# Up stage of a trunk layer: token blocks transposed before their sums, and three output sums of the early pairs on VectorE

## The chip, the cores and the metric

One NeuronCore of one Trainium2 chip runs the whole layer in a single launch. The metric is the device time of one execution, in microseconds (us). The time before the change is the median of three runs, 1518.04 us (1517.04 to 1518.28).

The engines are named as in the profile: PE is TensorE (PEld its weight load), DVE is VectorE, ACT is ScalarE, POOL is GpSimd, SP is SyncE, which here only issues DMAs.

## The reference, cut to what matters

One layer of a hybrid encoder: 16 meta tokens and 1024 tokens of width 1024. An input projection feeds neighbourhood attention and a gated recurrence; the two are merged, projected by `w_o`, and added to the residual stream. An MLP follows. The change lies between the two last steps:

```python
mix = jax.nn.sigmoid(gate_na) * y_na + jax.nn.sigmoid(gate_hg) * y_hg
h = h + mix @ w_o[l]
m = rms_norm(h, norm_mlp[l])
h = h + jnp.square(jax.nn.relu(m @ w_up[l])) @ w_down[l]
...
h = rms_norm(h, norm_final)
return h[:, N_META:]
```

`w_up` is 1024 x 4096 and `w_down` is 4096 x 1024; everything is float32. Only the 1024 token rows pass through these last steps.

## The kernel before, in words

**Precision.** Every large product is made from operands split into a rounded part `hi` (a cast on ACT) and a remainder `lo` (a subtraction on DVE), with three matmuls per block: hi·hi, hi·lo and lo·hi. In `chain` these are the lines L918, L919 and L920, twelve matmuls of 128x128 by 128x512 for one product.

**The `w_o` stage.** The token rows are eight blocks of 128 rows, `hres[0]` to `hres[7]`. `wo_rows(i, hc)` makes one half of a block's product with `w_o` (24 matmuls on L122 to L124) and adds it into `hres[i]` on DVE (L1216). `row_scale(i)` sends the sum to DRAM from the ACT queue (L1237, tile `hsp`), squares it on ACT (L1238) and makes the root on POOL (L92, L93). `scale_row(i)` multiplies the block in place on DVE (L1243); it has to wait until the DMA has read the old values.

**Winograd form.** The product with `w_up` is made in Strassen-Winograd form: the normalised rows, transposed, form a 2x2 grid of blocks `b11`, `b21` (rows 0 to 511, the two halves of the columns) and `b12`, `b22` (rows 512 to 1023). Beside these the scheme needs four sums, `t1` to `t4`. `row_sums(j)` makes those of block j and block j+4 from rows: two subtractions on DVE (L1249, L1250) and two on POOL (L1251, L1252). `to_variant` then transposes one 128x512 piece on PE (four transposes, L1259, into a PSUM bank `pt`), casts it from PSUM on ACT (L1261) and takes the remainder on DVE, again from PSUM (L1262). There are seven variants (`b11`, `b21`, `b22`, `t1` to `t4`) of four pieces each: 28 pieces and 112 transposes. The first eight pieces (`b11`, `b21`) are turned inside the `w_o` stage, the other twenty between the first products of the up stage. `b22` and `t2` go to a new tile `nT1`, which takes the place of the `w_o` operand `mT[1]`.

**The up stage.** `w_up` is taken in 16 pairs of 128-column blocks; a pair takes seven products, of one chain each. For pairs 0 to 2 ("early") the first two products are made ahead (`product_1` of the three, then `product_2` of the three), and the transposes above are laid between their matmuls. A pair's weights are its own sums on DVE (`pair_sums`, L908 to L911), then split by ACT (L1308) and DVE (L1309). The results go through relu and square on ACT (L1313, L1314), and `pair_out` with `finish_u2` makes four sums of them (`block_out`, L1401) for the next stage, on POOL except in the last pair, each followed by a DMA from SP (L1402). `load_pair` (L1335, SP) loads the weights of the pair after next.

**What sets the order.** In the `w_o` stage the framework's scheduler places the instructions. The up stage is under `manual_schedule`: there each engine runs in the order in which the code is written. All engines run in order and meet at semaphores.

Of the kernel before, what the change touches and what calls it, by code (L numbers as in the profile page):

```python
# [9 lines left out]
F32 = mybir.dt.float32  # L10
# [3 lines left out]
ALU = mybir.AluOpType  # L14
# [4 lines left out]
P = 128  # L19
# [3 lines left out]
TH = 512  # L23
# [25 lines left out]
def layer(ctx: ExitStack, tc: tile.TileContext, x, meta, w_in, w_na, w_hg, w_o, w_up, w_dn,  # L49
          g_mix, g_mlp, g_fin, gain, bias, lbl, lmask, wmask, out):  # L50
    nc = tc.nc
    pe, act, dve, pool, sp = nc.tensor, nc.scalar, nc.vector, nc.gpsimd, nc.sync
# [20 lines left out]
    def bank(tag, name):  # L73
        return banks[tag].tile([P, 4, P], F32, tag=tag, name=name)
# [4 lines left out]
    ident = cp.tile([P, P], F32, name="ident")  # L79
# [7 lines left out]
    def mm_tile(n=512, name="mm"):  # L87
        mm_cycle.append(mm_cycle.pop(0))
        return bank(mm_cycle[-1], name).rearrange("p a b -> p (a b)")[:, :n]
# [40 lines left out]
    def u_tiles(h, name):  # L130
        return [up.tile([P, KC, UW[h]], F32R, tag=f"u{h}{i}", name=f"{name}{h}{i}") for i in range(2)]
# [615 lines left out]
    with (tc.tile_pool(name="npr", bufs=1, side="right", reuse_waits="tile") as npr,  # L747
# [18 lines left out]
        for p in range(NPAIR):  # L766
            NB = npl.tile([P, 2, 1024], F32, tag="NB", name="NB")
            for i in range(2):
# [3 lines left out]
                for o, j0, m in ((0, 0, 3), (432, 1, 2), (720, 0, 2)):  # L772
                    a = NB[:, i, o:o + m * SW].rearrange("p (j c) -> p j c", c=SW)[:, :, :P]
                    pool.tensor_tensor(a, a, bs[:, j0 * P:(j0 + m) * P].rearrange("p (j c) -> p j c", c=P),
                                       op=ALU.subtract)
# [41 lines left out]
            for b in (0, 4, 8):  # L817
                pt = bank("t", "vpt")
                m = min(4, 9 - b)
                for j in range(m):  # L820
                    pe.transpose(pt[:, j], vT[:, b + j], ident)
                src = pt[:, :m].rearrange("p j (i d) -> p j i d", i=2)
# [331 lines left out]
    for br, wsrc in enumerate((w_hg, w_na)):  # L1154
        for jj in range(0, KC, 2):
            hi, lo = ahead_w.pop() if ahead_w else branch_weights(wsrc, jj)
            if br == 0 and jj == 2:
                list(branch_operand(1))
            for j in (jj, jj + 1):
# [4 lines left out]
                for h in range(2):  # L1164
                    pm = mm_tile()
                    t = slice(h * TH, (h + 1) * TH)
                    for k in range(4):
                        c = slice(k * 2 * P + (j - jj) * P, k * 2 * P + (j - jj + 1) * P)
# [33 lines left out]
    hres = [None] * 8  # L1202
# [39 lines left out]
    def scale_row(i, rs):  # L1242
        dve.scalar_tensor_tensor(hres[i], hres[i], rs, g2, op0=ALU.mult, op1=ALU.mult)  # L1243

    def row_sums(j):

        b11, b21, b12, b22 = (hres[i][:, q:q + TH] for i in (j, j + 4) for q in (0, TH))
        t2 = rowp.tile([P, TH], F32, tag="t2", name="t2", bufs=3)
        dve.tensor_tensor(b11, b12, b11, op=ALU.subtract)  # L1249
        dve.tensor_tensor(t2, b22, b11, op=ALU.subtract)  # L1250
        pool.tensor_tensor(b12, b22, b12, op=ALU.subtract)  # L1251
        pool.tensor_tensor(b21, b21, t2, op=ALU.subtract)  # L1252
        return {"t1": b11, "b22": b22, "t3": b12, "t2": t2, "t4": b21}

    def to_variant(tag, src, var, j):

        pt = bank(tag, "pt") if tag else mm_tile().rearrange("p (a b) -> p a b", a=4)
        for k in range(4):
            pe.transpose(pt[:, k], src[:, k * P:(k + 1) * P], ident)  # L1259
        hi = var[0][:, :, j * P:(j + 1) * P]  # L1260
        act.copy(hi, pt)  # L1261
        dve.tensor_tensor(var[1][:, :, j * P:(j + 1) * P], pt, hi.bitcast(F32), op=ALU.subtract)  # L1262

    for i in range(4):
        for hc in range(2):
            wo_rows(i, hc)
        scale_row(i, row_scale(i))
    nT0 = u_tiles(0, "nT")
    nV = {"b11": [t[:, :4, :TH] for t in nT0], "b21": [t[:, 4:, :TH] for t in nT0]}
    nB = []  # L1270
    for i in range(4, 8):
        for hc in range(2):
            wo_rows(i, hc)
        if i < 6:
            for j in (2 * i - 8, 2 * i - 7):
                to_variant("a", hres[j][:, :TH], nV["b11"], j)
                to_variant("a", hres[j][:, TH:], nV["b21"], j)
        if i < 7:
            scale_row(i, row_scale(i))
            if i > 4:  # L1280
                nB += [row_sums(j) for j in range(len(nB), i - 3)]
    wos.close()
    wps.close()


    ups = ExitStack()
    upw = ups.enter_context(tc.tile_pool(name="upw", bufs=1, reuse_waits="tile"))
    nT1 = u_tiles(1, "nT")
    nV["b22"], nV["t2"] = [t[:, :4, :TH] for t in nT1], [t[:, 4:, :TH] for t in nT1]
    nvp = ups.enter_context(tc.tile_pool(name="nvp", bufs=1, reuse_waits="tile"))  # L1290
    for v in ("t1", "t3", "t4"):
        nV[v] = [nvp.tile([P, 4, TH], F32R, name=f"n{v}{q}") for q in range(2)]
# [58 lines left out]
    def pair_sums(q):  # L1351
        raw = q.raw
        A = q.A = {"a11": raw[:, :4, :P], "a12": raw[:, 4:, :P], "a21": raw[:, :4, P:], "a22": raw[:, 4:, P:]}
        for v in ("s1", "s3"):
            t = a_tile(upw, "sx", bufs=2, n=D).rearrange("p (k c) -> p k c", c=P)
            A[v], A["s" + str(int(v[1]) + 1)] = t[:, :4], t[:, 4:]
        winograd(dve, *(A[v] for v in ("a11", "a12", "a21", "a22", "s1", "s2", "s3", "s4")))
# [12 lines left out]
    def product_1(q, w=None, between=lambda k: None, tag="pa"):  # L1370
        q.p1, q.u11 = a_tile(upa, "p1", bufs=EARLY), a_tile(upa, "u11", bufs=EARLY)
        q.pa = up_bank(tag)
        chain(q.pa, w or q.W["a11"], nV["b11"], True, between)
        act.copy(q.p1, q.pa)

    def product_2(q, w=None, between=lambda k: None):
        chain(q.pa, w or q.W["a12"], nV["b21"], False, between)
        relu2(q.u11, q.pa)
        (act if q.early or q.last else sp).dma_start(usp[0][q.m][:, 0], q.u11)
# [18 lines left out]

    def block_out(q, v, a, b, op, dst):
        q.S[v] = a_tile(upb, "us", bufs=4)  # L1400
        (dve if q.last else pool).tensor_tensor(q.S[v], a, b, op=op)  # L1401
        (pool if q.last else sp).dma_start(dst, q.S[v])  # L1402

    def product_7(q, then):
# [7 lines left out]
    def pair_out(q):  # L1412

        block_out(q, 2, q.u11, q.u1, ALU.subtract, usp[2][q.m][:, 1])
        block_out(q, 0, q.u1, q.u3, ALU.add, usp[1][q.m][:, 1])
        block_out(q, 1, q.S[0], q.u11, ALU.subtract, usp[1][q.m][:, 0])
# [16 lines left out]
    def last_first_weights(k):  # L1433
        if k == 2:
            first_w[2].append(weights(first_raw[2][:, 4:], upf))
# [6 lines left out]
    with tc.manual_schedule(engines={e.engine for e in (pe, act, dve, pool, sp)}):  # L1442

        rs7 = row_scale(7)
        count = [0]

        def transposes(n):
            for n in range(count[0], count[0] + n):
                v = ("t1", "b22", "t3", "t2", "t4")[n % 5]
                to_variant("a", nB[n // 5][v], nV[v], n // 5)  # L1450
                count[0] += 1

        product_1(pairs[0], first_w[0][0], lambda k: transposes(k > 0))
        first_weights(2, 0)
        transposes(2)
        scale_row(7, rs7)
        product_1(pairs[1], first_w[1][0], lambda k: transposes(1))
        transposes(1)
        nB.append(row_sums(3))
        product_1(pairs[2], first_w[2][0], lambda k: transposes(1), "mm")  # L1460
        transposes(2)
        product_2(pairs[0], first_w[0][1], lambda k: (transposes(1), last_first_weights(k)))
        rows_.close()
        hress.close()

        rawp = ups.enter_context(tc.tile_pool(name="rawp", bufs=1, side="right", reuse_waits="tile"))
        upr = ups.enter_context(tc.tile_pool(name="upr", bufs=1, side="right", reuse_waits="tile"))
        load_pair(0)
        load_pair(1)
        pair_sums(pairs[0])  # L1470
        product_2(pairs[1], first_w[1][1])
        next_weights(-1, "s4", "s2")
        product_2(pairs[2], first_w[2][1])
        early_w.close()
        psum_pools(pc=2, pb=2, pa=2)
        upb = ups.enter_context(tc.tile_pool(name="upb", bufs=1, reuse_waits="tile"))
        w_pools.insert(0, upr)
        next_weights(-1, "s1", "s3", "a22")
        for m, q in enumerate(pairs):
            if m + 2 < NP + 2:  # L1480
                load_pair(m + 2)
            (product_3 if q.early else product_1)(q)
            if m == 0:
                product_6(q)
            if m + 1 < NP:
                pair_sums(pairs[m + 1])
            if m:
                product_4(pairs[m - 1])
            if q.early:
                if m:  # L1490
                    product_6(q)
                next_weights(m, "a11", "s4")
                if m:
                    finish_u2(pairs[m - 1])
                next_weights(m, "a12", "s2", "s1")
            else:
                finish_u2(pairs[m - 1])
                product_3(q)
                next_weights(m, "a11", "s4")
                product_2(q)  # L1500
                next_weights(m, "a12", "s2")
                product_6(q)
                next_weights(m, "s1")
            product_5(q, lambda: next_weights(m, "s3"))
            product_7(q, lambda: next_weights(m, "a22"))
            if not q.last:
                pair_out(q)
        product_4(pairs[-1])
        finish_u2(pairs[-1])
        next_step()  # L1510
# [328 lines left out]
```

## Time and profile before

| | |
|---|---|
| median of three runs | 1518.04 us |
| the profiled execution, its own time | 1516.13 us |
| its span, first to last instruction | 1514.3 us |
| PE busy | 1499.2 us, 99% |
| DVE busy | 1033.6 us, 68% |
| ACT busy | 656.8 us, 43% |
| POOL busy | 381.7 us, 25% |
| mean granted clock of PE | 0.999 |
| `w_o` rows, first to last add (L1216) | 806.3 to 884.9 us of the span |
| early products and transposes | 884.0 to 909.7 us |
| early pairs, up to pair 3 | 909.7 to about 966 us |

A row of the timeline reads: start in us from the span's start, length in us, engine, line, operation, output and inputs by the program's names, shapes, and the count of merged instructions; in square brackets stands how long the engine had been idle, and what ended that. A row of the chain of waits has start, length and the line that time is put down to. A group's row has, behind the bar, busy us and mean ns of one, then the idle time before them. Matmuls overlap: one starts every 0.23 us though each shows 0.39 us, so distances between starts are what counts on PE.

### The profile page before, as it was taken

Reading aid. Unit: us, or ns where it says so; the run is one execution under the profiler, and the core shown is the slowest. Engines: PE = TensorE matmul, PEld = TensorE weight load, DVE = VectorE, ACT = ScalarE, POOL = GpSimd, SP = SyncE. Lnnn points to the kernel's source line nnn. Section 1 sums busy time; section 2 is a strip of 40 time slices with the busy share of each in tenths; the row PEclk is TensorE's granted clock in tenths of the full one; section 3 lists DMA queues with packets and bytes.
Section 4 is the critical chain, followed back from the end, with each engine's and each line's share of the span. In section 5 each row is a group of like instructions: output and inputs, shape, how many; then the busy total and the mean of one; then the engine's idle time right before and its main releaser. Section 6 shows DMA issues by size and latency. Waiting matters only on the chain.

```text
span 1514.3 us, 23574 instructions
## 1 busy us (share of the span) xinstructions
PE 1499.2 (99%) x9248; PEld 1255.7 (83%) x9248; DVE 1033.6 (68%) x1612; ACT 656.8 (43%) x1170; POOL 381.7 (25%) x358
## 2 busy tenths in 40 slices
PE   9999999999999999999999999999999999999998
PEld 8888888888888888888888887888888888888886
DVE  7876666656786796665584468877777445877876
ACT  7131313136575576344132145555555534334444
POOL 3313131324414400110000214444444200231142
PEclk9999999999999999999999999999999999999999
DMA  4211011113213237444655124544444576563224
GB/s 170 59 29 57 29 53 33 44 36 125 90 60 95 98 96 252 145 152 172 213 167 208 42 91 151 183 153 153 151 146 162 201 248 234 188 233 111 98 84 153
DMA packets 142590, 195.60 MB, mean 129 GB/s; under 512 B 8192, under 2 KB 90368, under 8 KB 142480
## 3 DMA queue, kind: packets, MB, share of 16 engines
q1 hardware_dynamic: 133072, 172.34, 34.4%
q10 hardware_dynamic: 7232, 14.44, 2.5%
q0 software_dynamic: 2176, 7.34, 1.3%
q8 instruction: 72, 1.18, 0.3%
q14 instruction: 38, 0.31, 0.1%
HBM read 139.56 MB, written 54.53 MB: 128 GB/s over the span
## 4 chain that ended last, share of the span: by engine, by line
PE 88%; DVE 6%; issue 2%; ACT 2%; DMA 1%; POOL 0%; POOLq 0%; ACTq 0%; DVEq 0%
PE mm L122 11%; PE mm L123 11%; PE mm L124 11%; PE mm L1514 4%; PE pa L1514 4%; PE pb L918 4%; PE pc L1514 4%; PE pb L919 4%; PE pb L1514 4%; PE pb L920 4%; PE pc L920 3%; PE pc L919 3%; PE pc L918 3%; PE pa L918 2%; PE pa L919 2%
## 5 line engine op out<-in xcount | busy, mean ns | idle before, releaser
L122 PE MATMUL mm<-aT,hi 128*128 128x512 f32 (+2 forms) x600 | 214.0, 357 | 0.0
L123 PE MATMUL mm<-aT,hi 128*128 128x512 f32 (+2 forms) x600 | 211.9, 353 | 0.0
L124 PE MATMUL mm<-aT,lo 128*128 128x512 f32 (+2 forms) x600 | 211.7, 353 | 0.0
L97 DVE TENSOR_TENSOR dl<-ur,dh 128x1024 fp32r<-128x1024 f32 x54 | 71.0, 1314 | 87.5 <-ACT dh L96 87.2
L96 ACT CAST dh<-ur 128x1024 fp32r<-128x1024 f32 x54 | 56.9, 1054 | 166.4 <-issue 91.1
L122 PEld LDWEIGHTS mm<-aT,hi 128*128 128x128 f32 x600 | 113.2, 189 | 12.6
L124 PEld LDWEIGHTS mm<-aT,lo 128*128 128x128 f32 x600 | 113.2, 189 | 12.4
L123 PEld LDWEIGHTS mm<-aT,hi 128*128 128x128 f32 x600 | 113.2, 189 | 12.0
L1309 DVE TENSOR_TENSOR wl<-raw,wh 128x512 fp32r<-128x512 f32 x50 | 41.3, 830 | 36.2 <-ACT wh L1308 36.1
L1313 ACT ACTIVATE uv<-uv 128x512 f32<-128x512 f32 x48 | 30.4, 633 | 80.0 <-DVE uv L1421 48.9
L1309 DVE TENSOR_TENSOR wl<-sx,wh 128x512 fp32r<-128x512 f32 x70 | 61.0, 882 | 5.2 <-ACT wh L1308 5.2
L1308 ACT CAST wh<-sx 128x512 fp32r<-128x512 f32 x70 | 42.2, 619 | 42.9 <-PE pc L919 23.9
L112 ACT CAST hi<-raw 128x1024 fp32r<-128x1024 f32 x26 | 27.3, 1051 | 77.2 <-PE mm L123 71.2
L1604 POOL TENSOR_TENSOR w<-w,tt 128x512 f32<-128x512 f32 x16 | 23.4, 1461 | 133.5 <-DVE tt L1603 112.7
L300 POOL TENSOR_TENSOR Y<-X,TN 128x512 f32<-128x512 f32 x20 | 34.2, 1712 | 83.4 <-DVE X L297 83.4
L844 DVE CUSTOM_DVE_ANT_0 pr<-nsc,NB 128x432 f32<-128x432 f32 (+1 forms) x64 | 35.2, 559 | 27.4 <-issue 20.0
L918 PE MATMUL pb<-nt,wh 128*128 128x512 f32 x128 | 50.4, 394 | 0.9 <-DVE uv L1391 0.7
L122 PE MATMUL mm<-wh,mT 128*128 128x512 f32 x128 | 50.1, 392 | 0.0
L124 PE MATMUL mm<-o,lo 128*128 128x512 f32 x128 | 49.9, 390 | 0.1
L919 PE MATMUL pb<-nt,wh 128*128 128x512 f32 x128 | 49.9, 390 | 0.0
L920 PE MATMUL pb<-nt,wl 128*128 128x512 f32 x128 | 49.8, 389 | 0.0
L124 PE MATMUL mm<-wh,mT 128*128 128x512 f32 x128 | 49.8, 389 | 0.0
(428 smaller groups left out, 4438.9 us busy)
## 6 DMA issues: line engine op xcount, KB each, us to landing
raw<-in_w_in SPq DMA_DIRECT2D x56, 512.0 KB, 4.1
ur<-usp SPq DMA_DIRECT2D x54, 512.0 KB, 3.4
raw<-in_w_up SPq DMA_DIRECT2D x16, 1024.0 KB, 6.1
usp<-us SPq DMA_DIRECT2D x60, 256.0 KB, 2.2
sg<-gsp SPq DMA_DIRECT2D x16, 512.0 KB, 5.0
w<-in_w_dn SPq DMA_DIRECT2D x16, 512.0 KB, 5.1
usp<-uv SPq DMA_DIRECT2D x30, 256.0 KB, 2.3
gsp<-gv ACTq DMA_DIRECT2D x24, 256.0 KB, 2.3
```

The lines of the kernel that those rows point to most:

```text
L96: act.copy(hi, src)
L97: dve.tensor_tensor(lo, src, hi.bitcast(F32), op=ALU.subtract)
L122: pe.matmul(ps, lh, rh, start=first, stop=False)
L123: pe.matmul(ps, lh, rl, start=False, stop=False)
L124: pe.matmul(ps, ll, rh, start=False, stop=last)
L844: dve.tensor_tensor_reduce(out=pr[:, :w], in0=sc[:, :w], in1=NB[:, i, o:o + w], scale=1.0, scalar=3.0e38, op0=ALU.add, op1=ALU.min, accum_ ...
L918: pe.matmul(ps, lhs[0][:, c], rhs[0][:, k], start=first and k == 0, stop=False, skip_group_check=True)
L919: pe.matmul(ps, lhs[0][:, c], rhs[1][:, k], start=False, stop=False, skip_group_check=True)
L920: pe.matmul(ps, lhs[1][:, c], rhs[0][:, k], start=False, stop=k == 3, skip_group_check=True)
L1308: act.copy(v(hi), src)
L1309: dve.tensor_tensor(v(lo), src, v(hi).bitcast(F32), op=ALU.subtract)
L1514: pe.matmul(ps, a[n == 2][:, q, j * P:(j + 1) * P], b[n == 1][:, q], start=first and n == 0, stop=last and n == 2, skip_group_check=True)
```

## The change

The rows are transposed first and summed after. `turn_half` transposes half a row block on PE, and `turn_back` copies the result from PSUM over the same half of `hres` (on ACT; for one half of row 7 on DVE). `row_sums` is unchanged but works on transposed halves, so its sums are already the wanted variants. `to_variant` only splits; for 20 of 28 pieces it reads `hres` or `t2` in SBUF instead of a PSUM bank. PE turns 16 halves, 64 transposes, instead of 112, and 16 copies are new. Rows 4 to 6 are turned, summed, and their `b22` and `t2` split, inside the `w_o` stage; these two variants are written over columns of `mT[1]` that `wo_rows` is done with. Row 7 is scaled and turned inside `product_1` of pair 1. In the early pairs `pair_out` is called one pair later, behind the next `pair_sums`, and its three sums run on DVE.

```diff
-    def to_variant(tag, src, var, j):
-
-        pt = bank(tag, "pt") if tag else mm_tile().rearrange("p (a b) -> p a b", a=4)
+    def by_block(t):
+        return t.rearrange("p (k c) -> p k c", c=P)
+
+    def to_variant(src, var, j):
+
+        hi, lo = (t[:, :, j * P:(j + 1) * P] for t in var)
+        act.copy(hi, src)
+        dve.tensor_tensor(lo, src, hi.bitcast(F32), op=ALU.subtract)
+
+    def turn_half(half):
+
+        pt = bank("a", "pt")
         for k in range(4):
-            pe.transpose(pt[:, k], src[:, k * P:(k + 1) * P], ident)
-        hi = var[0][:, :, j * P:(j + 1) * P]
-        act.copy(hi, pt)
-        dve.tensor_tensor(var[1][:, :, j * P:(j + 1) * P], pt, hi.bitcast(F32), op=ALU.subtract)
+            pe.transpose(pt[:, k], half[:, k * P:(k + 1) * P], ident)
+        return pt
+
+    def turn_back(half, eng, var=None, j=0):
+
+        pt = turn_half(half)
+        if var:
+            to_variant(pt, var, j)
+        (eng.copy if eng is act else eng.tensor_copy)(by_block(half), pt)
...
     for i in range(4, 8):
...
         if i < 6:
             for j in (2 * i - 8, 2 * i - 7):
-                to_variant("a", hres[j][:, :TH], nV["b11"], j)
-                to_variant("a", hres[j][:, TH:], nV["b21"], j)
+                turn_back(hres[j][:, :TH], act, nV["b11"], j)
+                turn_back(hres[j][:, TH:], act, nV["b21"], j)
         if i < 7:
             scale_row(i, row_scale(i))
-            if i > 4:
-                nB += [row_sums(j) for j in range(len(nB), i - 3)]
+            turn_back(hres[i][:, :TH], act)
+            turn_back(hres[i][:, TH:], act)
+            nB.append(row_sums(i - 4))
+            for v in ("b22", "t2"):
+                split_rows(v, i - 4)
...
-        (dve if q.last else pool).tensor_tensor(q.S[v], a, b, op=op)
+        (dve if q.last or q.early and v < 3 else pool).tensor_tensor(q.S[v], a, b, op=op)
...
-        product_1(pairs[0], first_w[0][0], lambda k: transposes(k > 0))
+        def last_row(k):
+            if k == 0:
+                scale_row(7, rs7)
+            elif k == 3:
+                turn_back(hres[7][:, :TH], dve)
+                turn_back(hres[7][:, TH:], act)
+                nB.append(row_sums(3))
+            else:
+                splits()
+
+        product_1(pairs[0], first_w[0][0], lambda k: splits(k > 0))
+        product_1(pairs[1], first_w[1][0], last_row)
         first_weights(2, 0)
-        transposes(2)
-        scale_row(7, rs7)
-        product_1(pairs[1], first_w[1][0], lambda k: transposes(1))
-        transposes(1)
-        nB.append(row_sums(3))
-        product_1(pairs[2], first_w[2][0], lambda k: transposes(1), "mm")
-        transposes(2)
-        product_2(pairs[0], first_w[0][1], lambda k: (transposes(1), last_first_weights(k)))
+        splits(2)
+        product_1(pairs[2], first_w[2][0], lambda k: splits(), "mm")
+        product_2(pairs[0], first_w[0][1], lambda k: (splits(k < 3), last_first_weights(k)))
...
             if m + 1 < NP:
                 pair_sums(pairs[m + 1])
+            if m and pairs[m - 1].early:
+                pair_out(pairs[m - 1])
             if m:
                 product_4(pairs[m - 1])
...
-            if not q.last:
+            if not (q.last or q.early):
                 pair_out(q)
```

The next rows are PE's order at the start of the up stage, before the change, in `product_1` of pair 0. `hres_8567` and `hres_8568` are row blocks 0 and 4, `pa` is the product's bank, `wh` and `wl` are weights.

```order
L918 MATMUL pa<-nT_8892,wh 128x512
L919 MATMUL pa<-nT_8893,wh 128x512
L920 MATMUL pa<-nT_8892,wl 128x512
L1259 MATMUL pt<-ident,hres_8567 128x128 x4
L918 MATMUL pa<-nT_8892,wh 128x512
L919 MATMUL pa<-nT_8893,wh 128x512
L920 MATMUL pa<-nT_8892,wl 128x512
L1259 MATMUL pt<-ident,hres_8568 128x128 x4
```

After the change the only transposes of the up stage are those of row block 7 (`hres_8566`), ahead of the last three matmuls of `product_1` of pair 1; the `mm` rows are `product_1` of pair 2.

```order
L918 MATMUL pa<-nT_8892,wh 128x512
L919 MATMUL pa<-nT_8893,wh 128x512
L920 MATMUL pa<-nT_8892,wl 128x512
L1268 MATMUL pt<-ident,hres_8566 128x128 x8
L918 MATMUL pa<-nT_8892,wh 128x512
L919 MATMUL pa<-nT_8893,wh 128x512
L920 MATMUL pa<-nT_8892,wl 128x512
L918 MATMUL mm<-nT_8892,wh 128x512
L919 MATMUL mm<-nT_8893,wh 128x512
L920 MATMUL mm<-nT_8892,wl 128x512
```

Twenty groups of four transposes have left this place, and one group of eight has come.

On DVE, before, the scaling of row block 7 (L1243 on `hres_8566`) and its sums (L1249 and L1250, with `hres_8565`, block 3) stand among remainders of turned pieces, read from PSUM (`pt`).

```order
L1243 SCALAR_TENSOR_TENSOR hres_8566<-hres_8566,rs,g_8646 128x1024
L1262 TENSOR_TENSOR nt_9212<-pt,nt_9211 128x4x128
L1262 TENSOR_TENSOR nT_9207<-pt,nT_9206 128x4x128
L1262 TENSOR_TENSOR nt_9214<-pt,nt_9213 128x4x128
L1262 TENSOR_TENSOR nT_9207<-pt,nT_9206 128x4x128
L1262 TENSOR_TENSOR nt_9216<-pt,nt_9215 128x4x128
L1249 TENSOR_TENSOR hres_8565<-hres_8566,hres_8565 128x512
L1250 TENSOR_TENSOR t_9370<-hres_8566,hres_8565 128x512
```

After, at the same place, three remainders of block 0 stand ahead of the scaling, and the copy of row 7's first half (L1276), its sums and the remainder of pair 2's first weights (L1329) behind it.

```order
L1262 TENSOR_TENSOR nt_9266<-hres_8567,nt_9265 128x4x128
L1262 TENSOR_TENSOR nt_9268<-hres_8568,nt_9267 128x4x128
L1262 TENSOR_TENSOR nt_9270<-hres_8567,nt_9269 128x4x128
L1243 SCALAR_TENSOR_TENSOR hres_8566<-hres_8566,rs,g_8646 128x1024
L1262 TENSOR_TENSOR nt_9266<-hres_8569,nt_9265 128x4x128
L1262 TENSOR_TENSOR nt_9268<-hres_8570,nt_9267 128x4x128
L1276 COPY hres_8566<-pt 128x512
L1249 TENSOR_TENSOR hres_8565<-hres_8566,hres_8565 128x512
L1250 TENSOR_TENSOR t_9368<-hres_8566,hres_8565 128x512
L1329 TENSOR_TENSOR wl<-sx,wh 128x512
```

The weights' remainder has moved behind row 7's chain, and the remainders read SBUF.

The third place is DVE in pair 1 of the up stage, from the sums of pair 2's weights on. Before (`p_9263` and `p_9319` are the first products of pairs 0 and 1, `uv` their results):

```order
L908 TENSOR_TENSOR sx<-raw 128x512
L909 TENSOR_TENSOR sx<-sx,raw 128x512
L910 TENSOR_TENSOR sx<-raw 128x512
L911 TENSOR_TENSOR sx<-raw,sx 128x512
L1421 TENSOR_TENSOR uv<-pb,p_9263 128x512
L1391 TENSOR_TENSOR uv<-pb,p_9319 128x512
```

After (`p_9317`, `p_9339` are the same first products; L1421 is now the line of `block_out`):

```order
L908 TENSOR_TENSOR sx<-raw 128x512
L909 TENSOR_TENSOR sx<-sx,raw 128x512
L910 TENSOR_TENSOR sx<-raw 128x512
L911 TENSOR_TENSOR sx<-raw,sx 128x512
L1421 TENSOR_TENSOR us<-u_9318,uv 128x512
L1421 TENSOR_TENSOR us<-uv 128x512
L1421 TENSOR_TENSOR us<-us,u_9318 128x512
L1441 TENSOR_TENSOR uv<-pb,p_9317 128x512
L1411 TENSOR_TENSOR uv<-pb,p_9339 128x512
```

Three output sums stand in DVE's queue between the weight sums and the two adds that read the product bank `pb`; they have left POOL's queue.

More of the change, by code (lines that the diff above doesn't have):

```diff
@@ L1267, in layer, with split_rows @@
         scale_row(i, row_scale(i))
-    nT0 = u_tiles(0, "nT")
-    nV = {"b11": [t[:, :4, :TH] for t in nT0], "b21": [t[:, 4:, :TH] for t in nT0]}
+    nT0, nT1 = u_tiles(0, "nT"), mT[1]
+    nV = {"b11": [t[:, :4, :TH] for t in nT0], "b21": [t[:, 4:, :TH] for t in nT0],
+          "b22": [t[:, :4] for t in nT1], "t2": [t[:, 4:] for t in nT1]}
     nB = []
+    def split_rows(v, j):
+        to_variant(by_block(nB[j][v]), nV[v], j)
     for i in range(4, 8):
@@ L1287, in layer @@
     upw = ups.enter_context(tc.tile_pool(name="upw", bufs=1, reuse_waits="tile"))
-    nT1 = u_tiles(1, "nT")
-    nV["b22"], nV["t2"] = [t[:, :4, :TH] for t in nT1], [t[:, 4:, :TH] for t in nT1]
     nvp = ups.enter_context(tc.tile_pool(name="nvp", bufs=1, reuse_waits="tile"))
@@ L1444, in layer, with splits @@
         rs7 = row_scale(7)
[L1445 to L1451, printed above, removed]
-        product_1(pairs[0], first_w[0][0], lambda k: transposes(k > 0))
-        first_weights(2, 0)
-        transposes(2)
-        scale_row(7, rs7)
-        product_1(pairs[1], first_w[1][0], lambda k: transposes(1))
-        transposes(1)
-        nB.append(row_sums(3))
-        product_1(pairs[2], first_w[2][0], lambda k: transposes(1), "mm")
-        transposes(2)
-        product_2(pairs[0], first_w[0][1], lambda k: (transposes(1), last_first_weights(k)))
+        todo = [(v, j) for j in range(3) for v in ("t1", "t3", "t4")]
+        todo += [(v, 3) for v in ("b22", "t2", "t1", "t3", "t4")]
+        def splits(n=1):
+            for _ in range(n):
+                split_rows(*todo.pop(0))
+        def last_row(k):
[9 more added lines that the diff above has]
+        product_1(pairs[1], first_w[1][0], last_row)
+        first_weights(2, 0)
+        splits(2)
+        product_1(pairs[2], first_w[2][0], lambda k: splits(), "mm")
+        product_2(pairs[0], first_w[0][1], lambda k: (splits(k < 3), last_first_weights(k)))
         rows_.close()
```

## Prediction

> **What bounds the kernel now.** I read the page's busy table and the chain's shares first, then the timeline of PE, DVE, ACT and POOL from 840 to 970 us.
>
> ```profile
> PE 1499.2 (99%) x9248; PEld 1255.7 (83%) x9248; DVE 1033.6 (68%) x1612; ACT 656.8 (43%) x1170; POOL 381.7 (25%) x358
> PE 88%; DVE 6%; issue 2%; ACT 2%; DMA 1%; POOL 0%; POOLq 0%; ACTq 0%; DVEq 0%
> ```
>
> PE bounds nearly everything, so a transpose that goes is worth its step on PE, as long as nothing PE waits for becomes late. Matmul steps are read from starts, transpose steps from the chain of waits.
>
> ```profile
> 842.74 0.39 PE L124 MATMUL mm<-wh,mT 128*128 128x512 f32 x1
> ...
> 847.50 0.39 PE L124 MATMUL mm<-wh,mT 128*128 128x512 f32 x1
> ...
> 888.62 1.31 PE pt L1259 x12
> ...
> L1259 PE MATMUL pt<-ident,hres 128*128 128x128 f32 x96 | 13.2, 274 | 0.1
> L1259 PE MATMUL pt<-ident,t 128*128 128x128 f32 x16 | 2.4, 272 | 0.0
> ```
>
> 21 matmuls lie between the first two rows: 4.76 / 21 = 0.227 us a step. Twelve transposes take 1.31 us of the chain: 0.109 each, though a row shows 0.27. There are 96 + 16 = 112.
>
> ```profile
> 884.05 0.39 PE L918 MATMUL pa<-nT,wh 128*128 128x512 f32 x1
> 909.71 0.39 PE L918 MATMUL pc<-nT,wh 128*128 128x512 f32 x1
> 910.24 0.50 PE L920 MATMUL pc<-nT,wl 128*128 128x512 f32 x1
> ...
> 931.48 0.39 PE L920 MATMUL pc<-nt,wl 128*128 128x512 f32 x1
> 932.17 0.50 PE L918 MATMUL pb<-nt,wh 128*128 128x512 f32 x1 [0.31 <-DVE uv L1391]
> ...
> 966.29 0.50 PE L918 MATMUL pb<-nt,wh 128*128 128x512 f32 x1 [0.24 <-DVE uv L1391]
> ```
>
> The up stage begins at 884.05; its six first products end at 909.71. That is 25.66 us = 72 x 0.227 + 80 x 0.109 + 0.6 of small gaps. From 909.71 to 966.29 PE makes 20 chains of 12 matmuls, 240 x 0.227 = 54.4, in 56.58: 2.2 us are lost. The step from 931.48 to 932.17 shows how: 0.69 in place of 0.23, because L1391, the read of the bank `pb`, comes late on DVE.
>
> ```profile
> 916.19 0.68 DVE L908 TENSOR_TENSOR sx<-raw 128x512 f32<-128x512 f32 x1
> ...
> 918.12 0.69 DVE L911 TENSOR_TENSOR sx<-raw,sx 128x512 f32<-128x512 f32 x1
> ...
> 923.39 1.30 POOL L1401 TENSOR_TENSOR us<-u,uv 128x512 f32<-128x512 f32 x1 [8.06 <-ACT uv L1314]
> 923.86 1.38 DVE L1309 TENSOR_TENSOR wl<-raw,wh 128x512 fp32r<-128x512 f32 x1
> 925.16 0.68 DVE L908 TENSOR_TENSOR sx<-raw 128x512 f32<-128x512 f32 x1
> 925.37 1.61 POOL L1401 TENSOR_TENSOR us<-uv 128x512 f32<-128x512 f32 x1 [0.68 <-ACT uv L1314]
> 925.87 1.66 DVE L909 TENSOR_TENSOR sx<-sx,raw 128x512 f32<-128x512 f32 x1
> 927.06 1.62 POOL L1401 TENSOR_TENSOR us<-us,u 128x512 f32<-128x512 f32 x1
> 927.45 1.77 DVE L910 TENSOR_TENSOR sx<-raw 128x512 f32<-128x512 f32 x1
> 928.64 1.73 POOL L1386 TENSOR_TENSOR uv<-p,uv 128x512 f32<-128x512 f32 x1
> 929.15 1.77 DVE L911 TENSOR_TENSOR sx<-raw,sx 128x512 f32<-128x512 f32 x1
> ...
> 931.45 0.68 DVE L1391 TENSOR_TENSOR uv<-pb,p 128x512 f32<-128x512 f32 x1
> ...
> 939.22 0.68 DVE L908 TENSOR_TENSOR sx<-raw 128x512 f32<-128x512 f32 x1
> ```
>
> The four weight sums take 2.6 us with POOL idle (916.19 to 918.81) and 5.7 us with three POOL operations among them (925.16 to 930.9). They alternate: L909 ends at 927.53, 0.55 after POOL's 926.98, and POOL, waiting, goes before L910.
>
> **The change, part by part. (1) Transposes.** 112 become 16 halves x 4 = 64: 48 x 0.109 = **-5.2 us** of PE. The up stage loses 80 and gets 8; the `w_o` stage gets 24 (+2.7 with restarts), which moves the up stage's start, T below, to about 886.8.
>
> **(2) Rows 4 to 6 in the `w_o` stage.** Each adds two copies, two casts and two remainders in a stretch where ACT and DVE are mostly idle. What can hurt is PE reaching a turn before the row is scaled.
>
> ```profile
> 874.09 0.33 ACTq L1237 DMA_DIRECT2D hsp<-hres  x1
> ...
> 877.92 1.29 DVE L1243 SCALAR_TENSOR_TENSOR hres<-hres,rs,g 128x1024 f32<-128x1024 f32 x1 [3.86 <-DMA hsp<-hres]
> ```
>
> For row 6 scaling ends 5.1 us after the DMA's issue; PE turns the row 25 matmuls (5.7 us) after the product's end, the add and the issue take some 0.9 of it, so PE can be 0.3 early. For rows 4 and 5 the same steps, with a shorter DMA wait, leave PE some 0.5 late, so no wait. Bounds 0 to 1.4 (what row 7 waits, below); I take **+0.2**.
>
> **(3) Row 7.** Here a new wait stands on PE.
>
> ```profile
> 884.25 0.69 DVE L1216 TENSOR_TENSOR hres<-hres,mm 128x512 f32<-128x512 f32 x1 [2.40 <-PE mm L124]
> ...
> 884.97 0.33 ACTq L1237 DMA_DIRECT2D hsp<-hres  x1
> 885.39 1.06 ACT L1238 ACTIVATE junk<-hres 128x1024 f32<-128x1024 f32 x1 [9.73 <-DVE hres L1216]
> ...
> 886.45 0.57 ACT L1261 CAST nt<-pt 128x512 fp32r<-128x512 f32 x1
> ...
> 889.13 0.62 ACT L1308 CAST wh<-sx 128x512 fp32r<-128x512 f32 x1
> ...
> 889.79 0.69 DVE L1309 TENSOR_TENSOR wl<-sx,wh 128x512 fp32r<-128x512 f32 x1 [0.53 <-ACT wh L1308]
> 891.60 1.27 DVE L1243 SCALAR_TENSOR_TENSOR hres<-hres,rs,g 128x1024 f32<-128x1024 f32 x1
> ```
>
> PE reaches the turn 21 matmuls after T: T+4.8. ACT's first free slot behind the square is T+2.4 (886.45); three casts at about 0.5, three remainders at 0.6 behind them (as 889.79 follows 889.13), then the scaling from T+4.85 to 6.1. PE waits 1.4. The turns (0.9) and three matmuls end at T+7.75, where pair 2's product needs its weights. Their cast stands on ACT behind the copy of row 7's second half and of pair 1's product: T+9.05. Their remainder stands on DVE behind two remainders, a copy and two sums, each 0.6 to 0.7, free at T+9.3. But POOL now makes row 7's differences:
>
> ```profile
> 896.50 0.69 DVE L1250 TENSOR_TENSOR t<-hres,hres 128x512 f32<-128x512 f32 x1
> 896.54 1.79 POOL L1251 TENSOR_TENSOR hres<-hres 128x512 f32<-128x512 f32 x1 [9.09 <-DVE hres L1249]
> 897.11 0.68 DVE L1262 TENSOR_TENSOR nt<-pt,nt 128x512 fp32r<-128x512 f32 x1
> ...
> 898.30 1.29 POOL L1252 TENSOR_TENSOR hres<-hres,t 128x512 f32<-128x512 f32 x1
> ```
>
> POOL starts right behind L1250 and ends 1.15 after it, at T+10.5; before, the next DVE operation read PSUM and was not held (0.68). Now it reads SBUF twice, as L1309 does at 923.86, and ends 0.55 after POOL: T+11.1. PE's third matmul, which needs it, would have started at T+8.2: 2.9 more. **+4.3 us** in all. Bounds: 0, if everything is early, and 5.6, if POOL's second difference also comes first (another 1.3); I take 4.3, from rows of the same operations. From there DVE has unbroken work to the weights of product 3 (another held remainder, nine operations at 0.6, four sums, one remainder), done at about T+22.1; PE arrives 48 matmuls after T+11.1, at T+22.0: a tie.
>
> So product 3's third matmul comes at 886.8 + 22.1 = 908.9, where it was 910.24: a gain of 1.3, which holds (1), (3) and the small gaps.
>
> [...]
>
> **(4) Output sums.** Per early pair DVE gets three operations, 3 x 0.68 = 2.0, and loses the stretch of three behind POOL: L1309 at 923.86 (0.7) and two of the three sums (2.1; the third still meets L1386). DVE falls from 14.1 (925.16 to 939.22, without a gap worth naming) to 13.3 us per pair, PE needs 60 x 0.227 = 13.6. Worked through in order, pair 1's read of `pb` ends 0.4 before PE comes, where it was 0.46 late; the next two come out 0.5 early and level. So of the 2.2 lost us, less 0.2 at 910.24, I take back **-1.8**. Bounds: 0 and -2.0. POOL keeps the fourth sum. The three DMAs per pair move on SP behind `load_pair`, which then issues earlier; the four `us` buffers cover them.
>
> Copies of turned halves (ACT 15, DVE 1) have the shape of the cast at 886.45, 0.57; they are hidden behind matmuls except in (3), where they are counted.
>
> **The sum.** -1.3 + 0.2 - 1.8 = -2.9 us. Against the profiled execution's 1516.13 that is 1513.2. The median of three is 1518.04, 1.9 above that execution, so I forecast a median of **1515.1**. A measurement of this kernel can tell about 0.2% from no change, 3.0 us: the forecast sits on that line.
>
> **The rivals.**
> *A. Row 7 waits less.* If POOL's difference comes after the remainder, or the casts run quicker, (3) shrinks. For it speaks that ACT and DVE have gaps there; against, that every row is in order behind row 7's scaling. The gain is 4.2 (1513.8) without POOL's block and at most 7 or so, with no wait at all. Chance 0.17.
> *B. DVE or the turns eat the rest.* The tie at product 3 falls to DVE, or the rows of the `w_o` stage wait up to 1.4: gain 0.3 to 1.8, about 1517. For it: two near ties in the working. Chance 0.14.
> *C. Slower.* The place is DVE in the early pairs. If its long sums don't come from POOL's `block_out`, they stay at 1.7 and the three added sums come on top: 2.05 x 3 = 6.15 later at 966 us, where DVE already is late, less the 1.3 gained: +4.9, 1522.9. It decides once DVE needs over 13.6 us per pair. Against it stand 2.6 us with POOL idle, and ends that fall 0.55 behind POOL's. Chance 0.11.
>
> **How the numbers follow.** The forecast has 0.58, its own range 1513.8 to 1516.2, half on either side of 0.2%. Faster: 0.29 + 0.17 = 0.46; same: 0.29 + 0.14 = 0.43; slower: 0.11. The range leaves out C and the far end of A: 1512.4 to 1518.0.
>
> **What would show it.** Right: 64 transposes; a PE wait of about 1.4 on L1243 at row 7's turn, one of about 2.9 on L1329 in pair 2's first product with POOL L1251 beside it; no PE waits on L1411 or L1426 in pairs 1 to 3; L909 to L911 at 0.69 except one per pair. Wrong: PE waiting at turns of rows 4 to 6, a PE wait at product 3 of pair 0 of over 0.3, or waits for `pb` that stay.

## The result, and the profile after

The changed kernel takes 1514.19 us, the median of nine runs (1511.24 to 1516.2), beside 1517.13 us before, also of nine (1516.48 to 1518.28): 2.94 us less, a ratio of 0.9978 with a 95% interval of 0.9969 to 0.9987. A second series of ten runs gave 1513.87 beside 1516.87 (0.9982, 0.9972 to 0.9991). The change makes the kernel faster, by about 0.2%.

The profiled execution took 1511.24 us, its span is 1509.5 us at a mean granted clock of 0.999. The busy table and the shares of the chain, from the page of the changed kernel:

```profile
PE 1492.1 (99%) x9200; PEld 1250.8 (83%) x9200; DVE 1035.8 (69%) x1622; ACT 665.0 (44%) x1185; POOL 370.7 (25%) x349
PE 92%; DVE 4%; issue 2%; ACT 2%; POOL 0%; DMA 0%; POOLq 0%; ACTq 0%; DVEq 0%
```

PE has 48 matmuls fewer (9248 to 9200), the transposes that went; the chain runs through PE more than before.

The span is 4.8 us shorter than before's, which is more than the runs gained. Two executions also differ in places that the change doesn't touch, so I compare distances between three landmarks: the second add of row block 4 (L1216 on DVE), the third matmul of product 3 of pair 0 (the first L920 on `pc`), and the first block sum of pair 4 (L1391 before, L1411 after, on DVE). The timeline of DVE has the outer two. Before:

```profile
847.93 0.69 DVE L1216 TENSOR_TENSOR hres<-hres,mm 128x512 f32<-128x512 f32 x1 [4.76 <-PE mm L124]
983.24 0.68 DVE L1391 TENSOR_TENSOR uv<-pb,p 128x512 f32<-128x512 f32 x1
```

After:

```profile
846.71 0.69 DVE L1216 TENSOR_TENSOR hres<-hres,mm 128x512 f32<-128x512 f32 x1 [4.76 <-PE mm L124]
...
978.84 0.68 DVE L1411 TENSOR_TENSOR uv<-pb,p 128x512 f32<-128x512 f32 x1
```

With product 3 at 910.24 before and 907.93 after (next fence), the **first stretch** goes from 62.31 to 61.22 us (-1.09), the **second** from 73.00 to 70.91 (-2.09): 3.18 us in all. Of the other 1.6 us of the span, 1.22 (847.93 less 846.71) arise ahead of the changed code, and the changed kernel's own second profile (e10) stands at 849.93 there. The last 0.4 lie behind pair 4, mostly near 1294 us, where PE waits once for a remainder (L97 on DVE; a step of 0.61 us in place of 0.23, at 1294.17) in the profile of before and in none of the others.

PE's timeline at the start of the up stage, after the change; the bracket is PE's idle time and what ended it:

```profile
885.69 0.39 PE L918 MATMUL pa<-nT,wh 128*128 128x512 f32 x1
...
891.82 1.09 PE L1268 MATMUL pt<-ident,hres 128*128 128x128 f32 x8 [1.21 <-DVE hres L1243]
...
894.80 0.50 PE L918 MATMUL mm<-nT,wh 128*128 128x512 f32 x1 [1.19 <-ACT wh L1328]
...
896.83 0.50 PE L920 MATMUL mm<-nT,wl 128*128 128x512 f32 x1 [1.30 <-DVE wl L1329]
...
907.93 0.50 PE L920 MATMUL pc<-mT,wl 128*128 128x512 f32 x1
```

The stage starts at 885.69. The three brackets are new: PE waits for row 7 to be scaled, for the cast of pair 2's first weights, and for their remainder. They are all that PE waits for in the region, as the view of waits from 840 to 970 us says (time in all, times, longest), first before, then after:

```profile
PE pb L918 <- DVE uv L1391: 0.7, 3, 0.3
PE pb L918 <- DVE uv L1406: 0.2, 1, 0.2
```

```profile
PE mm L920 <- DVE wl L1329: 1.3, 1, 1.3
PE pt L1268 <- DVE hres L1243: 1.2, 1, 1.2
PE mm L918 <- ACT wh L1328: 1.2, 1, 1.2
```

Four waits for the bank `pb` have gone, and three for row 7 and the weights have come. Behind the latter stand DVE and POOL; their timelines in the changed kernel:

```profile
890.48 1.28 DVE L1243 SCALAR_TENSOR_TENSOR hres<-hres,rs,g 128x1024 f32<-128x1024 f32 x1
...
893.60 0.69 DVE L1249 TENSOR_TENSOR hres<-hres,hres 128x512 f32<-128x512 f32 x1
894.40 0.69 DVE L1250 TENSOR_TENSOR t<-hres,hres 128x512 f32<-128x512 f32 x1
895.01 1.77 DVE L1329 TENSOR_TENSOR wl<-sx,wh 128x512 fp32r<-128x512 f32 x1
```

```profile
894.44 1.79 POOL L1251 TENSOR_TENSOR hres<-hres 128x512 f32<-128x512 f32 x1 [5.40 <-DVE hres L1249]
...
923.53 1.78 POOL L1406 TENSOR_TENSOR uv<-p,uv 128x512 f32<-128x512 f32 x1 [10.58 <-issue]
```

POOL's difference, released by L1249, ends at 896.23; the weights' remainder (L1329) takes 1.77 in place of 0.69 and ends 0.55 behind it. In the early pairs, where the same kind of hold had made three DVE sums long (1.66, 1.77 and 1.77 us in place of 0.69), only one is left, beside POOL's L1406 above:

```profile
922.87 0.69 DVE L909 TENSOR_TENSOR sx<-sx,raw 128x512 f32<-128x512 f32 x1
923.49 0.68 DVE L910 TENSOR_TENSOR sx<-raw 128x512 f32<-128x512 f32 x1
924.09 1.78 DVE L911 TENSOR_TENSOR sx<-raw,sx 128x512 f32<-128x512 f32 x1
...
928.31 0.68 DVE L1411 TENSOR_TENSOR uv<-pb,p 128x512 f32<-128x512 f32 x1
```

### The profile page after: what moved, and what is told of

Its sections match the earlier page's. It is cut to its first block, busy times and chain, and to the rows that moved or that the text cites. A ratio compares the mean times of both kernels' runs of the same rounds, so it can differ in the third digit from the quotient of the medians.

```text
span 1509.5 us, 23492 instructions
## 1 busy us (share of the span) xinstructions
PE 1492.1 (99%) x9200; PEld 1250.8 (83%) x9200; DVE 1035.8 (69%) x1622; ACT 665.0 (44%) x1185; POOL 370.7 (25%) x349
## 4 chain that ended last, share of the span: by engine, by line
PE 92%; DVE 4%; issue 2%; ACT 2%; POOL 0%; DMA 0%; POOLq 0%; ACTq 0%; DVEq 0%
PE mm L122 11%; PE mm L123 11%; PE mm L124 11%; PE mm L1541 5%; PE pa L1541 5%; PE pb L918 4%; PE pb L919 4%; PE pb L920 4%; PE pb L1541 4%; PE pc L1541 4%; PE pc L920 3%; PE pc L919 3%; PE pc L918 3%; PE pa L920 2%; PE pa L919 2%
## 5 line engine op out<-in xcount | busy, mean ns | idle before, releaser
L97 DVE TENSOR_TENSOR dl<-ur,dh 128x1024 fp32r<-128x1024 f32 x54 | 70.0, 1297 | 87.0 <-ACT dh L96 85.2
L1329 DVE TENSOR_TENSOR wl<-sx,wh 128x512 fp32r<-128x512 f32 x70 | 62.1, 897 | 3.6 <-ACT wh L1328 3.6
L1329 DVE TENSOR_TENSOR wl<-raw,wh 128x512 fp32r<-128x512 f32 x50 | 39.0, 783 | 36.4 <-ACT wh L1328 36.3
L123 PE MATMUL mm<-wl,mT 128*128 128x512 f32 x128 | 50.1, 391 | 0.0
L918 PE MATMUL pb<-nt,wh 128*128 128x512 f32 x128 | 49.9, 390 | 0.0
L123 PE MATMUL mm<-o,hi 128*128 128x512 f32 x128 | 49.8, 389 | 0.0
```

The costliest lines, as they stand in the source:

```text
L97: dve.tensor_tensor(lo, src, hi.bitcast(F32), op=ALU.subtract)
L123: pe.matmul(ps, lh, rl, start=False, stop=False)
L918: pe.matmul(ps, lhs[0][:, c], rhs[0][:, k], start=first and k == 0, stop=False, skip_group_check=True)
L1329: dve.tensor_tensor(v(lo), src, v(hi).bitcast(F32), op=ALU.subtract)
```

## The experiments

The theory: the change has two independent parts. Turning ahead takes 5.2 us of transposes away and gives most of it back in the three waits; the output sums give 2 us, because they no longer hold DVE's sums from POOL. Each part is tried alone (e1, e2), the second is taken apart (e3, e9), the three waits are attacked one by one (e4 to e7), and the runs' spread is looked at (e8, e10). The table gives both stretches of every profile; they don't depend on what an execution loses elsewhere. A ratio is to runs of before in the same series, with medians of 1517.3 (e1 to e4), 1516.55 (e5 to e8) and 1516.87 (e9, e10), so between rows the ratios are to be compared and not the medians.

| kernel | row 4's add | product 3 | pair 4 | first stretch | second | median (runs) | ratio to before |
|---|---|---|---|---|---|---|---|
| before | 847.93 | 910.24 | 983.24 | 62.31 | 73.00 | 1517.13 (9) | 1 |
| changed | 846.71 | 907.93 | 978.84 | 61.22 | 70.91 | 1514.19 (9) | 0.9978 [0.9969, 0.9987] |
| e1 turning alone | 847.57 | 908.80 | 981.76 | 61.23 | 72.96 | 1516.62 (11) | 0.9995 [0.9986, 1.0004] |
| e2 output sums alone | 847.72 | 910.06 | 980.96 | 62.34 | 70.90 | 1513.92 (11) | 0.9981 [0.9973, 0.999] |
| e3 late, on POOL | 848.05 | 910.87 | 982.43 | 62.82 | 71.56 | 1515.31 (10) | 0.9987 [0.9978, 0.9996] |
| e4 weights ahead | 849.03 | 910.20 | 981.14 | 61.17 | 70.94 | 1512.87 (10) | 0.9975 [0.9966, 0.9984] |
| e5 differences on DVE | 847.47 | 910.38 | 981.28 | 62.91 | 70.90 | 1513.88 (10) | 0.9981 [0.9972, 0.999] |
| e6 both | 849.50 | 909.64 | 980.52 | 60.14 | 70.88 | 1511.74 (6) | 0.997 [0.9959, 0.9981] |
| e7 remainders ahead too | 847.64 | 906.63 | 977.57 | 58.99 | 70.94 | 1510.63 (5) | 0.9961 [0.9949, 0.9974] |
| e8 filled waits | 847.63 | 908.88 | 979.79 | 61.25 | 70.91 | 1512.09 (6) | 0.9972 [0.996, 0.9984] |
| e9 old place, on DVE | 848.26 | 909.45 | 980.43 | 61.19 | 70.98 | 1513.05 (10) | 0.9975 [0.9965, 0.9985] |
| e10 changed again | 849.93 | 911.15 | 982.09 | 61.22 | 70.94 | 1513.87 (10) | 0.9982 [0.9972, 0.9991] |

**e1, turning alone.** The output sums go back to POOL and to the pair's end.

```diff
-        (dve if q.last or q.early and v < 3 else pool).tensor_tensor(q.S[v], a, b, op=op)
+        (dve if q.last else pool).tensor_tensor(q.S[v], a, b, op=op)
...
-            if m and pairs[m - 1].early:
-                pair_out(pairs[m - 1])
...
-            if not (q.last or q.early):
+            if not q.last:
                 pair_out(q)
```

> The change without its second part: the early pairs' output sums are back on POOL and back at their old place. Two stretches are read from the profile: A, from the second add of row block 4 (DVE) to the third matmul of product 3 of pair 0 (before 62.31 us, changed kernel 61.22), and B, from there to the read of the product bank by pair 4's u1 add (before 73.00, changed 70.91). Theory (the two parts add, the waits in the early pairs come from POOL holding DVE up): A 61.2, B 73.0, so 1.1 us faster than before. Rival (the earlier start of the pairs alone takes the waits away): A 61.2 and B about 71.

The first stretch is the changed kernel's, the second is that of before, and the view of waits adds to the three waits the ones for the bank `pb`:

```profile
PE pb L918 <- DVE uv L1411: 0.7, 3, 0.3
```

In time this kernel can't be told from before: 1516.62 beside 1517.3, and the interval, -2.1 to +0.6 us, holds both nothing and the trace's 1.1 us. Turning ahead, the larger part of the diff, is worth 1.1 us in the trace and nothing that the runs' times can show. A part of this lies outside the kernel's span: the times of e1's runs are 2.1 to 2.2 us above their spans, those of before 1.7 to 1.8. The medians of the spans are 1514.5 and 1515.5, 1.0 apart.

**e2, output sums alone.** The same three edits of `block_out`, `pair_out` and its place, made in the kernel of before.

> The kernel before with the second part alone: pair_out of the early pairs behind the next weight sums, its three sums on DVE; transposes as before. Theory: A 62.3, B 70.9, so 2.1 us faster than before, with no PE wait on the read of pb in pairs 1 to 3. Rival (the gain in B needs the turned blocks of the first part): B 73.

The first stretch is that of before, the second the changed kernel's, and the view of waits between 840 and 985 us is empty. The ratio, 0.9981, is as good as that of the whole change; its interval, 1.5 to 4.1 us gained, holds the trace's 2.1. In the stretches the parts add up: 62.34 less 61.22 and 72.96 less 70.91 are the two gains, each with the other part left as it was. The runs are too coarse to show this sum.

**e3, late but on POOL.** The changed kernel with POOL as the engine of the output sums, at the new place.

```diff
-        (dve if q.last or q.early and v < 3 else pool).tensor_tensor(q.S[v], a, b, op=op)
+        (dve if q.last else pool).tensor_tensor(q.S[v], a, b, op=op)
```

> The changed kernel with the early pairs' output sums called at their new, later place, but on POOL. It tells the engine from the place. Theory (POOL's reads hold DVE): the POOL sums now stand beside the weight remainders of the next pair, which also read SBUF twice, so DVE is stretched there and B stays between 72 and 73. Rival (only the place matters, because the sums no longer stand beside the weight sums): B 70.9 as in the changed kernel. A 61.2 by both.

The expectation missed: the second stretch came to 71.56. The place alone gives 1.44 of the 2.09 us. In pairs 1 and 2 POOL now makes the output sums behind DVE's four weight sums instead of among them; in pair 3 it still makes them among these (L909 and L910 take 1.67 and 1.78), and one wait for `pb` is left. The first stretch was 1.6 us longer than in the changed kernel, with the same three waits. The windows behind them show why; the columns are the stretch and its length, busy time of PE, PEld, DVE, ACT and POOL, and then the granted clock (PEclk):

```profile
899.20:902.60 3.40, 3.40 (x9) 2.64 (x8) 3.40 (x6) 0.58 (x2) 0.06 (x1) 0.51 0.45 108
902.60:906.00 3.40, 3.40 (x16) 2.82 (x15) 3.06 (x6) 2.97 (x7) 0.00 (x0) 1.00 0.56 200
```

For 3.4 us PE ran at half its clock and made 8 to 9 matmuls where the next 3.4 us have 16. This comes back below.

**e9, old place but on VectorE.** The other half of that pair: the sums on DVE, at the pair's end as before.

```diff
             if m + 1 < NP:
                 pair_sums(pairs[m + 1])
-            if m and pairs[m - 1].early:
-                pair_out(pairs[m - 1])
...
-            if not (q.last or q.early):
+            if not q.last:
                 pair_out(q)
```

> The changed kernel with VectorE making the early pairs' three output sums, but at their old place, at the pair's end. Engine and place together gave 2.09 us between product 3's third matmul and pair 4's first sum (73.00 to 70.91), the place alone 1.44 (71.56). If the engine is worth its 0.65 only on top of the place, this stretch stays near 72.3 to 73.0; if either of them is enough to free the waiting products, it comes to 71.0 to 71.6. The first stretch is the changed kernel's, 61.2 us.

The second stretch is 70.98, all but 0.07 of the gain. The timeline of DVE in pair 1 of this kernel:

```profile
925.24 1.69 DVE L1421 TENSOR_TENSOR us<-us,u 128x512 f32<-128x512 f32 x1
926.85 0.68 DVE L908 TENSOR_TENSOR sx<-raw 128x512 f32<-128x512 f32 x1
927.56 0.69 DVE L909 TENSOR_TENSOR sx<-sx,raw 128x512 f32<-128x512 f32 x1
928.17 0.69 DVE L910 TENSOR_TENSOR sx<-raw 128x512 f32<-128x512 f32 x1
928.77 0.68 DVE L911 TENSOR_TENSOR sx<-raw,sx 128x512 f32<-128x512 f32 x1
```

One output sum is held by POOL's L1406 (1.69 us, beside 925.08 to 926.37 on POOL), and all four weight sums are short. So engine and place are two ways to the same end, POOL off the weight sums. The place gets two thirds of it, the engine nearly all, and the new place adds only 0.07 us to the engine.

**e4, weights ahead.** Of the three waits, two are for pair 2's first weights. Here these are split right behind row 7's scaling.

```diff
             if k == 0:
                 scale_row(7, rs7)
+                first_weights(2, 0)
...
-        first_weights(2, 0)
         splits(2)
```

> The changed kernel with pair 2's first weights split right behind row 7's scaling instead of behind its sums, so that PE finds them ready. It takes away the two waits of PE at product 1 of pair 2 (1.36 and 1.47 us in the changed kernel's profile). Theory: DVE's queue, unbroken from the first remainders to the weights of product 3, sets the end of stretch A together with PE; the order within it does not matter, so A stays at 61.1 to 61.3 and the wait turns up at product 3 of pair 0. Rival (PE's waits are the price by themselves): A falls by 2.8 to 58.4.

The first stretch didn't move (61.17). The waits did; from the view of waits:

```profile
PE mm L920 <- DVE wl L1329: 1.7, 1, 1.7
PE pt L1268 <- DVE hres L1243: 1.2, 1, 1.2
PE pc L918 <- ACT wh L1328: 0.6, 1, 0.6
```

The wait of the first row now stands at pair 2's second product, 906.29 us, where I had looked for it at product 3 alone. DVE's unbroken work up to product 3's weights sets the end, and PE waits for it earlier or later.

**e5, differences on VectorE.** Row 7's two differences, which held the remainder, go from POOL to DVE.

```diff
-    def row_sums(j):
+    def row_sums(j, eng=pool):
...
-        pool.tensor_tensor(b12, b22, b12, op=ALU.subtract)
-        pool.tensor_tensor(b21, b21, t2, op=ALU.subtract)
+        eng.tensor_tensor(b12, b22, b12, op=ALU.subtract)
+        eng.tensor_tensor(b21, b21, t2, op=ALU.subtract)
...
-                nB.append(row_sums(3))
+                nB.append(row_sums(3, dve))
```

> The changed kernel with row 7's two differences (POOL in row_sums, 1.8 us each beside DVE) on DVE, 0.6 each. Stretches A and B as before: 61.22 and 70.91 in the changed kernel. Theory (PE and DVE tie at the end of stretch A; POOL's hold lengthens DVE by 2.2 and this adds 1.2): DVE alone gets 1.0 shorter, but the weights of product 1 of pair 2 come no earlier, because two sums now stand before them, so PE's wait there stays and A stays at 61.2 to 61.4. Rival (POOL's hold is what A costs): A falls by 1 or more, to 60.2.

The remainder is short now, and as late, behind the two differences. The timeline of DVE:

```profile
895.72 0.68 DVE L1251 TENSOR_TENSOR hres<-hres 128x512 f32<-128x512 f32 x1
896.32 0.68 DVE L1252 TENSOR_TENSOR hres<-hres,t 128x512 f32<-128x512 f32 x1
896.92 0.68 DVE L1329 TENSOR_TENSOR wl<-sx,wh 128x512 fp32r<-128x512 f32 x1
```

The waits are those of the changed kernel to 0.1 us. The first stretch, 62.91, again holds about 3.4 us at half clock (matmul steps of 0.43 from 897.66 to 901.2, 1.65 us lost); without these it would be 61.3, as expected.

**e6, both.** e4's and e5's edits together.

> Both edits that each alone should change nothing: pair 2's first weights right behind row 7's scaling, and row 7's differences on DVE. Theory (two chains, PE's wait for the weights and DVE's queue, end together, so that only both edits help): A falls by the 1.0 that DVE gets shorter, to 60.2; B 70.9. Rival (the edits add up by themselves, as far as each alone gave something): A 61.2.

60.14: the two edits, each worth nothing alone, give 1.1 us together, and the median is 1511.74, 4.8 below before's of its series. The weights ahead take the waits from pair 2; the differences on DVE shorten the unbroken work behind them.

**e7, remainders ahead too.** The wait at row 7's turn is left. In e6's kernel, the three splits ahead of row 7's scaling go ahead of its square on ACT.

```diff
-        rs7 = row_scale(7)
...
-        product_1(pairs[0], first_w[0][0], lambda k: splits(k > 0))
+        splits(3)
+        rs7 = row_scale(7)
+        product_1(pairs[0], first_w[0][0])
```

> As with both edits, and the casts and remainders of block 0 (three of each) stand ahead of row 7's DMA and square, not behind them. Two of the casts can then run during the last w_o product, and the scaling of row 7 waits for its DMA and root alone, 1.1 us earlier (add to scaling 3.45 us, 4.59 in the changed kernel). Theory (DVE's queue from the scaling on sets A): A falls by another 1.1, to 59.1; PE's wait at row 7's turn from 1.2 to about 0.2; time 1.5 to 2.5 us below the changed kernel's. Rival (PE is the bound by then): A stays at 60.2.

The turn's wait falls to 0.2 us (a matmul at 891.13 with a step of 0.23, the turn at 891.56), and the view of waits holds two rows:

```profile
PE mm L920 <- DVE wl L1329: 0.7, 1, 0.7
PE pc L918 <- ACT wh L1328: 0.6, 1, 0.6
```

The first stretch is 58.99, 3.3 us shorter than before. The median, 1510.63 (1510.03 to 1511.99), is 5.9 us below before's of its series, where the changed kernel gained 2.9 and 3.0, and all five runs lie below the lowest of e10's ten (1512.49).

**e8, filled waits.** The changed kernel's runs spread over 5 us, before's over 1.8. The trace of e3 showed half clock behind the waits; here PE fills them with matmuls.

```diff
+        def fill(n):
+            ps = up_bank("a") if n else None
+            for _ in range(n):
+                pe.matmul(ps, first_w[0][0][0][:, :P], nV["b11"][0][:, 0], start=True, stop=True)
...
             elif k == 3:
+                fill(5)
                 turn_back(hres[7][:, :TH], dve)
...
-        product_1(pairs[2], first_w[2][0], lambda k: splits(), "mm")
+        product_1(pairs[2], first_w[2][0], lambda k: (fill(11 if k == 0 else 0), splits()), "mm")
```

> The changed kernel with idle matmuls, whose results are never read, laid into PE's three waits in the early products: 5 ahead of row 7's turn, 11 ahead of product 1 of pair 2 (0.227 us each, 3.6 us in 4.2 of waiting). They take away PE's idle time and leave the order. Theory of the spread: in one run (late, but on POOL) 8 matmul steps right behind these waits took 0.43 instead of 0.227, so PE's clock was halved for 3.4 us and 1.6 us were lost; in the changed kernel this happens in some runs and not in others, which spreads them over 5 us. With the waits filled no run has a mean clock below 0.999, A stays at 61.2, and the median falls by 1 to 2 us below the changed kernel's 1514.2. Rival (the spread has another source): the same spread and the same median.

The stretches are unchanged, one wait of 0.3 us is left, and the ratio, 0.9972, is lower than the changed kernel's (0.9978 and 0.9982), but the intervals overlap. Five of six runs lie within 0.9 us, but three show a mean clock of 0.998, where I expected none, and one took 1515.06. That is no better a share than with the waits (35 of 60, below). So the median speaks for the theory that the waits cost clock, the listed clocks speak against it, and six runs don't settle it.

**e10, the changed kernel again.**

> The changed kernel itself, for its profile a second time and its runs on this chip. The stretches are 61.2 and 70.9 us, unless the half-rate steps seen in two of the variants with the same three waits fall into the profile; then the first is 1.6 us longer. The median is 1513 to 1515.5, with the runs spread over 3 us or more, if the three waits cost clock in a part of the runs; under 1.5 us of spread would speak against that.

The stretches are the same to 0.03 us. The runs spread over 2.6 us (1512.49 to 1515.13), between my two marks, and those of before over as much in this series (1515.68 to 1518.29). This profile, too, holds a half-clock stretch, at another place. Its windows at the start of the launch:

```profile
5.00:7.70 2.70, 1.36 (x16) 1.12 (x14) 1.96 (x4) 2.30 (x4) 1.34 (x2) 1.00 1.06 394
7.70:11.20 3.50, 3.50 (x20) 3.47 (x19) 2.39 (x7) 2.94 (x5) 1.78 (x3) 0.52 1.13 349
11.20:14.00 2.80, 2.80 (x27) 2.80 (x27) 1.27 (x2) 0.40 (x1) 0.00 (x0) 0.99 1.03 419
```

There PE waits 1.34 us for the first rows to be scaled (L573 on DVE), in code that both kernels share. So not all of the changed kernel's spread comes from the three waits.

## Why the prediction was right

The sum was -2.9 us, the runs show -2.94 (-3.0 in the second series). That these agree to 0.04 us is luck: the interval goes from 2.0 to 4.7 us, and the two stretches of the profiles gained 3.18. What bears the prediction out is the terms, read in the stretches. The forecast of 1515.1 lies 0.9 above the median measured, since it stood on a median before of 1518.04 from three runs; nine gave 1517.13.

**Terms (1) to (3), at product 3.** With the +0.2 of term (2), a gain of 1.1 was foreseen, and 1.09 came. The transposes are 64, and the up stage starts 2.86 us later against row 4's add (36.12 to 38.98), where 2.75 and 0.2 were expected; none of the turns of rows 4 to 6 waits. At row 7's turn PE waits 1.21 by the trace, 1.37 longer than a step would take; predicted was 1.4. For pair 2's weights it loses 1.36 and 1.47, together 2.83; predicted was 2.9. I had named one wait, on the remainder; about half of it came first, on the cast, which the same working has at T+9.05, 1.3 behind PE. POOL's hold is there as predicted, 0.55 included, but e4 and e5 show that removing the hold or the weights' late place alone gains nothing: what decides is the unbroken work on DVE up to product 3's weights, where I had a tie, and a tie it was. The prediction's rival A (POOL's block gone, 4.2 us gained in place of 2.9) thus priced the block as if nothing stood behind it. No run shows these 1.3 us as a gain of their own: e5, which takes the block away, has a first stretch of 62.91, about 61.3 without its half clock, beside 61.22.

**Term (4).** -1.8 foreseen, -2.09 measured. Pair 1's read of `pb` ends 0.4 us before PE comes, as worked out (928.99, PE at 929.39), and the weight sums are short except one. Mis-sized by 0.3 is the rest: I took 0.2 off for a last read that came out level with PE, and it cost nothing; my far bound of 2.0 was 0.09 short. The cause, POOL's output sums holding DVE's weight sums, is shown by e9 from one side and e3 from the other: with POOL away e9's four sums take 0.68 to 0.69 us each, and beside POOL's output sums two of e3's in pair 3 take 1.67 and 1.78. These sums have two inputs in SBUF. In pair 1 of e3 an add with one input in PSUM, L1441 at 928.72, took 0.68 beside POOL's L1421 (928.21, 1.75 us long).

**What was not foreseen.** The new waits may cost clock. The mean granted clock of a run is listed to three digits, and 0.001 of 1510 us is 1.5 us, about what one half-clock stretch cost (1.6 us in e3, 1.65 in e5). The twelve profiles fit this: the three with such a stretch amid PE's work (e3, e5, e10) are listed at 0.998, the nine others at 0.999. Of the 60 runs of kernels with all three waits (changed, e1, e3, e5, e9, e10), 25 stand at 0.999; of 102 runs without them (70 of before, and e2, e4, e6, e7), 84 do. e8, in neither count, has 3 of 6. The nine first runs of the changed kernel differ in time by it: five at 0.999 have a mean of 1512.62 us, four at 0.998 of 1515.26. The mark is not exact: the profiles of before and of the changed kernel also end with 2.8 and 2.6 us at a granted clock of 0.50 in which PE has no work left, some 0.001 of the mean by themselves, and e8's quickest run (1511.26) stands at 0.998. Lost clock may be another part of why e1's 1.1 us don't show in time. Where a run without a trace lost its clock stays open, and that the waits are the cause is not shown.

## What to carry to other kernels

Work taken off the bounding engine counts only as far as the next input is there: 5.2 us of transposes gave 1.1, because the rows and weights behind them came no earlier, and two edits that each gained nothing gave 1.1 us together. Where the trace shows VectorE's operations stretched beside GpSimd's (here sums with two inputs in SBUF, 1.66 to 1.78 us in place of 0.69), move GpSimd's away from those that somebody waits for; here another engine did it nearly in full (70.98 us beside 70.91) and another time for two thirds (71.56). Compare distances between landmarks on both sides of a change before reading spans: here 1.6 us of the span's 4.8 had nothing to do with it.

## What was not expected of the hardware

Three waits of 1.2 to 1.4 us each within some 6 us, with matmuls between, were followed in two of six such profiles (e3, e5) by 3.4 us at half clock (0.51 in e3), and in four (changed, e1, e9, e10) by none. None of the six profiles without all three (before, e2, e4, e6, e7, e8) shows it there; two of six beside none of six can still be chance. At the start of e10 PE was idle for 1.3 us and then ran at half clock; the idle stretches of 0.6 (changed), 1.2 (e3) and 1.4 us (e2) at that place were not followed by it (a granted clock of 1.00 there), so the length of one such stretch doesn't decide. The lengths at half clock were alike, 3.4 us in e3 and e5 and 3.5 in e10; the longest single wait ahead of that in e3 was 1.30 us. What starts such a stretch and what sets its length is not shown.
